# Shift and scale columns of w_ada in two halves, x normed by row before it is transposed, and the scan's state part summed by token

## The chip, the cores and the metric

The program runs on one core of a Trainium2 chip. The metric is the device time of one execution, in microseconds (us); lower is better. The engines are TensorE (PE, with its weight loads as PEld), VectorE (DVE), ScalarE (ACT), GpSimd (POOL) and SyncE (SP, which here issues most transfers).

## The reference, cut to what matters

One layer of a diffusion backbone: 512 latent tokens `x` and 256 context tokens `ctx`, width 1024.

```python
def _rmsnorm(x, g):
    xf = xf * lax.rsqrt(jnp.mean(xf * xf, axis=-1, keepdims=True) + NORM_EPS)
    return xf * g
def _modulate(x, g, shift, scale):
    return _rmsnorm(x, g) * (1 + scale) + shift
...
sh1, sc1, ga1, sh2, sc2, ga2 = split(silu(c) @ w_ada + b_ada, 6)      # and csh1, csc1, ... from c_ctx
p  = _modulate(x,   n_pre_mix, sh1,  sc1)  @ w_in      # q, k, v, z, xbc, dt, gates
pc = _modulate(ctx, n_pre_mix, csh1, csc1) @ w_in
...
# SSD scan, both directions, per group g of 8 heads, chunks c of 128 tokens:
y_diag = einsum('bcgls,bcgrls,bcsgrp->bclgrp', cb, Lm, x)             # inside a chunk
y_off  = einsum('bclgn,bcgrpn,bcgrl->bclgrp', Cc, h_prev, exp(a_cs))  # from the state
y = y_diag + y_off
```

The scan is followed by neighbourhood attention, two branch projections merged by gates, an output projection with a gated residual, and 16 routed SwiGLU experts with a second gated residual. Everything is float32.

## The kernel before, in words

**Tiling.** Products of the projections run as three float32r passes: each operand is cut into a high and a low part (`hh`, `hl` for the latent tokens, `ch`, `cl` for the context, `wh`, `wl` for the weights), and `gemm_k` adds high x high, low x high and high x low over 8 steps k of 128 channels into a PSUM tile of one output tile (128 columns of `w_in` by 512 tokens, or by 256 of the context).

**The opening.** The first lines load x and ctx (`load_xin`, six tiles of 128 tokens), the parts of `w_ada` that hold shift and scale (`load_ada`, 8 tiles q of 128 channels each) and the first columns of `w_in` (`load_first`: dt with 64 columns, B and C with 128). The string START is the order in which SP issues them: x, a and f for the three. NXIN and NWADA are the buffers of the first two. A row of x in SBUF stands in the scan's order of tokens, made by the load (`x_src`). The constants `cn` and the vectors `vec` come over POOL's queue. Each tile of x is squared and summed by row (L305 on DVE for odd tiles, ACT for even), transposed by PE (L310) and copied into `xT`, channels by tokens. `rsq` makes the reciprocal roots `rsv` by ten small DVE instructions (L183 to L188). Since tokens now lie along the free axis, `rsv` is spread over all partitions by matmuls with a diagonal (L318 to L320) into `rsb`, and POOL multiplies `xT` by it, 16 times (L327 to L329).

Then a loop over q = 0 to 7, the k steps of the first three output tiles: eight matmuls of `silu(c)` with the 256 columns of `w_ada` (L336), a copy (L339), two matmuls that select the rows of c and c_ctx and turn them (L342), bias and scale (L345, L347) into `mod`; DVE applies them to `xT` (L351), ACT casts the high part (L352), DVE subtracts for the low part (L353), and `gemm_k` runs for the three tiles (L214 to L222).

**The scan.** Four groups g of heads, two halves hf of 4 heads, four chunks c. `step_states` makes the states `hp` (PE L580, DVE L582 and L584). `step_chunk` makes one chunk of one half: POOL masks the log decays into `dd` (L595), ACT takes exponentials (L599), PE multiplies C with the states (L603), DVE adds the directions (L606), scales the state part of both into `tt` (L608) and weights the inner part by `cbs` (L610). In the tile `py` of PSUM, PE then adds up four matmuls that turn `tt` by the identity, one per direction and pair of heads (L614), and four of the inner part (L618). ACT copies it (`ys`, L622), and SP stores it. The projections and convolutions of group g + 1 (L481, L489) are mixed with this.

**What sets the order.** A scheduler orders each engine's instructions ahead of the run, from the order in which the program is written, from priorities (`high_priority` with the HP_ constants) and from buffer counts. PSUM has pools `pT` (transposes), `pY` (one buffer), `pS` and `mm`. Each engine then runs its list in order and waits where an operand is not there.

## Time and profile before

| | us |
|---|---|
| median of 3 runs (lowest, highest) | 2117.17 (2114.04, 2117.47) |
| profiled execution, own time | 2113.9 |
| its span | 2111.8 |
| PE busy, share of the span | 1950.3, 92% |
| DVE | 899.1, 43% |
| ACT | 636.6, 30% |
| POOL | 293.4, 14% |

The span is from the first to the last recorded event of the profiled execution; its own time is 2.1 us more. Read by stages, with the time that PE was busy in each:

| stage | from, to | PE busy | granted clock |
|---|---|---|---|
| opening | 0, 40 | 18.57 of 40 | 0.95 |
| | 40, 53 | 9.85 of 13 | 0.50 |
| | 53, 80 | 27.00 of 27 | 1.00 |
| first convolutions | 80, 148 | 65.82 of 68 | 0.97 |
| scan, with later projections | 148, 446 | 294.74 of 298 | 1.00 |
| start of the attention | 446, 480 | 29.89 of 34 | 0.90 |
| attention | 480, 780 | 285.16 of 300 | 1.00 |
| gates, branches, merge | 780, 1090 | 302.49 of 310 | 0.98 |
| experts | 1090, 2111.8 | 916.82 of 1021.8 | 0.95 |

"Busy" says that an engine had an instruction under way, not that it could go no faster. The clock is what the throttle granted TensorE: 1.00 is 2.4 GHz, 0.50 is 1.2 GHz. In the rows, a line with x16 is a group of like instructions with its busy time and the mean of one; in a timeline the first number is the start, the second the time that the group was busy, and the bracket the idle time of the engine ahead of it, with what ended it.

### The profile page before, as it was taken

What the parts mean: (1) busy time and instruction counts of PE and PEld (TensorE: products, weight loads), DVE (VectorE), ACT (ScalarE), POOL (GpSimd) and SP (SyncE); (2) the same over time, 40 slices, a digit from 0 to 9 for tenths busy, and PEclk for the clock granted to TensorE, in tenths of its full rate; (3) what the DMA queues carried; (4) which work ended last, traced back from release to release, by engine and by line L of the source; (5) the groups of instructions that cost most, each with busy time, mean ns of one, the idle gap of its engine ahead of it and who ended that gap; (6) DMA issues with size and microseconds to landing.
All of it is one profiled execution on the core that took longest, in us unless ns stands there. A gap on an engine that the chain in (4) does not pass through costs nothing.

```text
span 2111.8 us, 26456 instructions
## 1 busy us (share of the span) xinstructions
PE 1950.3 (92%) x10643; PEld 1268.6 (60%) x10643; DVE 899.1 (43%) x1612; ACT 636.6 (30%) x1263; POOL 293.4 (14%) x386
## 2 busy tenths in 40 slices
PE   5999999999999999999997899999998989899895
PEld 3777787777777777788887434444444334444342
DVE  5787777746666657743336201111111111111113
ACT  2465556435555554542222011100101001010102
POOL 3032213233343323310000000000000000000001
PEclk8999999999999999999998899999999999999998
DMA  9344234342332334454365799999999999999996
GB/s 242 95 133 140 81 119 145 105 142 93 112 117 100 113 106 155 150 175 132 112 249 208 310 393 423 428 428 427 428 427 427 428 428 427 428 426 428 427 428 252
DMA packets 143226, 548.39 MB, mean 260 GB/s; under 512 B 10520, under 2 KB 96584, under 8 KB 116992
## 3 DMA queue, kind: packets, MB, share of 16 engines
q1 hardware_dynamic: 127648, 490.10, 58.6%
q0 software_dynamic: 15024, 55.29, 7.8%
q8 instruction: 84, 1.38, 0.3%
q10 hardware_dynamic: 432, 1.31, 0.2%
q14 instruction: 38, 0.31, 0.0%
HBM read 529.72 MB, written 16.94 MB: 259 GB/s over the span
## 4 chain that ended last, share of the span: by engine, by line
PE 64%; DMA 12%; DVE 8%; issue 4%; ACT 3%; POOL 1%; DVEq 0%; POOLq 0%; ACTq 0%; SPq 0%
PE pu L1229 17%; DMA wb<-in_w_exp_down 7%; PE pd L1272 6%; PE ps_mm L214 4%; PE ps_mm L215 4%; PE ps_mm L220 4%; PE px L1184 3%; PE px L1279 2%; PE ps_mm L935 2%; PE ps_mm L934 2%; PE ps_mm L933 2%; DMA wc<-in_w_exp_up 2%; PE ps_y L614 1%; PE ps_t L798 1%; DMA wc<-in_w_exp_down 1%
## 5 line engine op out<-in xcount | busy, mean ns | idle before, releaser
L214 PE MATMUL ps_mm<-hh,wh 128*128 128x512 f32 (+1 forms) x648 | 265.8, 410 | 10.0 <-DVE sz L920 7.5
L215 PE MATMUL ps_mm<-hl,wh 128*128 128x512 f32 (+1 forms) x648 | 261.6, 404 | 2.6 <-DVE hl L353 2.6
L220 PE MATMUL ps_mm<-hh,wl 128*128 128x512 f32 (+1 forms) x648 | 261.7, 404 | 0.0
L168 DVE TENSOR_TENSOR wl<-raw,wh 128x1024 fp32r<-128x1024 f32 (+2 forms) x109 | 141.7, 1300 | 197.5 <-ACT wh L167 193.2
L167 ACT CAST wh<-raw 128x1024 fp32r<-128x1024 f32 (+2 forms) x109 | 117.1, 1074 | 196.2 <-PE ps_mm L934 84.7
L1229 PE MATMUL pu<-wb,xg 128*64 128x512 f32 x752 | 170.9, 593 | 0.0
L214 PEld LDWEIGHTS ps_mm<-hh,wh 128*128 128x128 f32 (+1 forms) x648 | 123.4, 190 | 44.8 <-issue 17.0
L1171 DVE SCALAR_TENSOR_TENSOR yo<-pd,gs,yo 64x512 fp32r<-64x512 f32 (+1 forms) x34 | 24.4, 718 | 281.2 <-ACT yo L1169 280.6
L215 PEld LDWEIGHTS ps_mm<-hl,wh 128*128 128x128 f32 (+1 forms) x648 | 123.3, 190 | 20.7 <-DVE hl L353 3.1
L220 PEld LDWEIGHTS ps_mm<-hh,wl 128*128 128x128 f32 (+1 forms) x648 | 123.4, 190 | 16.0 <-issue 0.8
L1229 PEld LDWEIGHTS pu<-wb,xg 128*64 128x64 f32 x752 | 75.5, 137 | 81.4 <-issue 54.3
L1211 POOL DMA_DIRECT2D g<-gain_scr x1 | 0.5, 528 | 868.7 <-PE pu L1229 868.7
L1252 DVE SCALAR_TENSOR_TENSOR hid<-hid,pu 128x512 f32<-128x512 f32 x32 | 22.0, 687 | 224.1 <-ACT hid L1251 224.1
L481 DVE SCALAR_TENSOR_TENSOR cacc<-pad,cwh,cacc 128x772 f32<-128x772 f32 (+1 forms) x96 | 100.4, 1050 | 9.6 <-ACT cacc L479 8.6
L1251 ACT ACTIVATE hid<-pu 128x512 f32<-128x512 f32 x32 | 19.0, 597 | 257.8 <-PE pu L1229 257.8
L1169 ACT ACTIVATE yo<-pd,gs 64x512 fp32r<-64x512 f32 (+1 forms) x34 | 22.3, 657 | 232.7 <-PE pd L1272 208.9
L1272 PE MATMUL pd<-wb,hidT 128*64 128x512 f32 x352 | 79.8, 597 | 12.9 <-DMA wb<-in_w_exp_down 12.9
L1279 PE MATMUL px<-yo,ohT 128*128 128x512 f32 x120 | 57.0, 577 | 35.0 <-DVE yo L1171 34.6
L217 PE MATMUL ps_mm<-ch,wh 128*128 128x256 f32 x280 | 82.2, 293 | 4.1 <-ACT rw L684 4.0
L599 ACT ACTIVATE dd<-dd,lnb 128x128 f32<-128x128 f32 x256 | 79.7, 392 | 10.3 <-POOL dd L595 9.9
L222 PE MATMUL ps_mm<-ch,wl 128*128 128x256 f32 x280 | 81.0, 289 | 0.0
L218 PE MATMUL ps_mm<-cl,wh 128*128 128x256 f32 x280 | 80.7, 288 | 0.0
(837 smaller groups left out, 3717.5 us busy)
## 6 DMA issues: line engine op xcount, KB each, us to landing
wb<-in_w_exp_gate SPq DMA_DIRECT2D x31, 2048.0 KB
wb<-in_w_exp_down SPq DMA_DIRECT2D x22, 2048.0 KB
raw<-in_w_in SPq DMA_DIRECT2D x36, 1024.0 KB
wa<-in_w_exp_gate SPq DMA_DIRECT2D x16, 2048.0 KB
wc<-in_w_exp_up SPq DMA_DIRECT2D x16, 2048.0 KB
ws<-in_w_exp_gate SPq DMA_DIRECT2D x16, 2048.0 KB
wr<-in_w_exp_up SPq DMA_DIRECT2D x16, 2048.0 KB
wb<-in_w_exp_up SPq DMA_DIRECT2D x16, 2048.0 KB
```

The lines of the kernel that those rows point to most:

```text
L167: S.copy(wh, v[:, :, c0:c0 + n])
L168: eng.tensor_tensor(wl, v[:, :, c0:c0 + n], wh.bitcast(F32), op=OP.subtract)
L214: PE.matmul(lat, wh[:, k, :m], hh[:, k, :], start=s, stop=False)
L215: PE.matmul(lat, wh[:, k, :m], hl[:, k, :], start=False, stop=False)
L217: PE.matmul(ctxp, wh[:, k, :m], ch[:, k, :], start=s, stop=False)
L218: PE.matmul(ctxp, wh[:, k, :m], cl[:, k, :], start=False, stop=False)
L220: PE.matmul(lat, wl[:, k, :m], hh[:, k, :], start=False, stop=e)
L222: PE.matmul(ctxp, wl[:, k, :m], ch[:, k, :], start=False, stop=e)
L481: E.scalar_tensor_tensor(acc[:, :n], pad[:, j:j + n], w(j), acc[:, :n], op0=OP.mult, op1=OP.add)
L1229: PE.matmul(acc[q * 2 + b][o * 64:(o + 1) * 64, :], xe[:, k, :], w[:, f:f + 512], start=(k == 0), stop=(k == KT - 1))
L1272: PE.matmul(pd[dh * 64:(dh + 1) * 64, :], l, wd[:, q * 1024 + dh * 512:q * 1024 + (dh + 1) * 512], start=(n == 0), stop=(n == 15))
L1279: PE.matmul(p, ohT[:, i * 128:(i + 1) * 128], yo[:, dh], start=True, stop=True)
```

## The change

It has two parts.

**Opening.** x is loaded in token order, one transfer per tile; `vec` and `cn` come over ACT's queue. Of the two halves u of the channels (512 each) `load_ada` fetches 8 tiles, with rows of 512 columns (2 KB) in place of 128 (512 B), each tile two k steps deep. The x tiles are scaled by `rsv` by row, in pairs, before their transposes (DVE even, ACT odd tiles); `rsb`, its diagonals and POOL's multiplies are gone. `columns(u)` makes `mod` for four q at a time, at q = 0 and q = 4: 16 matmuls with 512 columns into one tile of `pY`, one copy, four selecting matmuls, bias and scale. The scan's order of tokens is now made where DVE applies the modulation (a new tile `hq`); ACT applies that of the context.

**Scan.** DVE adds the two directions of `tt`, PE transposes the sum into a tile of its own (`pt`, pool `pT`), `py` holds the inner part alone, ACT copies `pt` into `ys` and DVE adds `py` to it.

```diff
-NXIN = 4
-NWADA = 6
-START = "xxxxafxxafafaaaaa"
+NXIN = 6
+NWADA = 5
+START = "xxxxxxaaaafffaaaa"
...
-    G.dma_start(vec, a["vec"])
-    G.dma_start(cn, a["cn"])
+    S.dma_start(vec, a["vec"])
+    S.dma_start(cn, a["cn"])
...
-        if i < 4:
-            for q in range(2):
-                nc.sync.dma_start(t[q * 64:(q + 1) * 64, :], x_src[2 * i + q])
...
+        nc.sync.dma_start(t, a["x"][i * 128:(i + 1) * 128, :] if i < 4 else a["ctx"][(i - 4) * 128:(i - 3) * 128, :])
...
-    def load_ada(q):
-        r = st.tile([128, KT, 2, 128], F32, name="wada", tag="wada", bufs=NWADA)
+    def load_ada(n):
+        u, k = n // 4, n % 4 * 2
+        r = st.tile([128, 2, 2, 512], F32, name="wada", tag="wada", bufs=NWADA)
         for v in range(2):
-            nc.sync.dma_start(r[:, :, v, :], a["w_ada"][:, v * 1024 + q * 128:v * 1024 + (q + 1) * 128]
+            nc.sync.dma_start(r[:, :, v, :], a["w_ada"][k * 128:(k + 2) * 128, v * 1024 + u * 512:v * 1024 + (u + 1) * 512]
                               .rearrange("(k p) n -> p k n", p=128))
...
-    V.tensor_copy(cb[:, 0:128], ident)
...
-    for i0, n in ((0, 4), (4, 2)):
-        rsq(rsv[:, i0:i0 + n], ssq[:, i0:i0 + n], 1.0 / D, EPS, st)
-        p = pT((128, n * 128))
-        for i in range(n):
-            dg = st.tile([128, 128], F32, name="dg", tag="dg", bufs=2)
-            V.tensor_scalar(dg, ident, rsv[:, i0 + i:i0 + i + 1], None, op0=OP.mult)
-            PE.matmul(p[:, i * 128:(i + 1) * 128], ones, dg, start=True, stop=True)
-        S.copy(rsb[:, i0 * 128:(i0 + n) * 128], p)
+        if i % 2 == 0:
+            continue
+        rsq(rsv[:, i - 1:i + 1], ssq[:, i - 1:i + 1], 1.0 / D, EPS, st)
+        for j in (i - 1, i):
+            if j % 2:
+                S.activation(xin[j], xin[j], AF.Copy, scale=rsv[:, j:j + 1])
+            else:
+                V.tensor_scalar(xin[j], xin[j], rsv[:, j:j + 1], None, op0=OP.mult)
+            for b in range(2):
+                p = pT()
+                for k in range(4):
+                    PE.transpose(p[:, k * 128:(k + 1) * 128], xin[j][:, (b * 4 + k) * 128:(b * 4 + k + 1) * 128], ident)
+                d = xT[:, b * 4:(b + 1) * 4, j * 128:(j + 1) * 128]
+                (S.copy if b else V.tensor_copy)(d, p.rearrange("p (k n) -> p k n", k=4))
...
-    for k in range(KT):
-        for sl in (slice(0, T), slice(T, T + TC)):
-            G.tensor_tensor(xT[:, k, sl], xT[:, k, sl], rsb[:, sl], op=OP.mult)
...
+    def columns(u):
+        with tc.high_priority(offset=HP_ADA):
+            p = pY()
+            for k in range(KT):
+                for v in range(2):
+                    i = k % 2 * 2 + v
+                    PE.matmul(p[i * 32:(i + 1) * 32, :], sil[:, k, :], wada[u * 4 + k // 2][:, k % 2, v],
+                              start=(k < 2), stop=(k >= 6))
+            row = st.tile([128, 512], F32, name="row", tag="row", bufs=1)
+            S.copy(row, p)
+            p = pT((128, 4, 2, 2))
+            for b in range(4):
+                PE.matmul(p[:, b].rearrange("p s v -> p (s v)"), row[:, b * 128:(b + 1) * 128], cn[:, C_SEL:C_SEL + 4],
+                          start=True, stop=True)
...
     for q in range(KT):
...
+        if q % 4 == 0:
+            columns(q // 4)
         for v, sl, hi, lo in ((0, slice(0, T), hh, hl), (1, slice(T, T + TC), ch, cl)):
...
-            V.tensor_scalar(t, t, sc_, sh_, op0=OP.mult, op1=OP.add)
+            if v == 0:
+                t = st.tile([128, T], F32, name="hq", tag="hq", bufs=2)
+                V.tensor_scalar(split_hrc(t), perm_hrc(src), sc_, sh_, op0=OP.mult, op1=OP.add)
+            else:
+                t = src
+                S.activation(t, src, AF.Identity, scale=sc_, bias=sh_)
...
+            V.tensor_tensor(tt[:, 0], tt[:, 0], tt[:, 1], op=OP.add)
+            pt = pT((128, 2, 128))
+            for pr in range(2):
+                PE.transpose(pt[:, pr, :], tt[:, 0, pr * 2:pr * 2 + 2, :].rearrange("p h e -> p (h e)"), ident)
             py = pY((128, 2, 128))
             for pr in range(2):
-                for d in range(2):
-                    PE.matmul(py[:, pr, :], tt[:, d, pr * 2:pr * 2 + 2, :].rearrange("p h e -> p (h e)"), ident,
-                              start=(d == 0), stop=False)
                 for o in range(2):
...
-                              start=False, stop=True)
+                              start=True, stop=True)
             ys = sdl.tile([128, 2, 128], F32, name="ys", tag="ys", bufs=2)
-            S.copy(ys, py)
+            S.copy(ys, pt)
+            V.tensor_tensor(ys, ys, py, op=OP.add)
```

Two places show how the order of the instructions moves. The first is PE's list from its start to the first matmul of the projection (L214). Before, with L310 the transposes, L319 the diagonals, L336 the columns and L342 the selection:

```order
L310 MATMUL ps_t<-cn,xin 128x128 x32
L336 MATMUL ps_y<-wada,sil 32x256 x8
L310 MATMUL ps_t<-cn,xin 128x128 x16
L319 MATMUL ps_t<-dg,cn 128x128 x4
L336 MATMUL ps_y<-wada,sil 32x256 x8
L319 MATMUL ps_t<-dg,cn 128x128
L342 MATMUL ps_t<-cn,row 128x2 x2
```

After, from the last transposes (L311) on, with L330 the columns and L336 the selection:

```order
L311 MATMUL ps_t<-cn,xin 128x128 x8
L330 MATMUL ps_y<-wada,sil 32x512 x4
L336 MATMUL ps_t<-cn,row 128x4 x4
L330 MATMUL ps_y<-wada,sil 32x512
L214 MATMUL ps_mm<-hh,wh 64x512
```

The columns of the first half are finished and selected in one piece, ahead of the projection. Those of the second half are strewn between its first steps; their four selecting matmuls stand once more, ahead of the fifth step.

The second place is PE's list at the first chunks of the scan. Before, L603 is C with the states, L614 and L618 fill `py`:

```order
L603 MATMUL ps_s<-hp,cT 128x256 x3
L222 MATMUL ps_mm<-ch,wl 128x256
L614 MATMUL ps_y<-cn,dd 128x128 x2
L618 MATMUL ps_y<-dd,xs_tok 64x128 x2
L614 MATMUL ps_y<-cn,dd 128x128 x2
L618 MATMUL ps_y<-dd,xs_tok 64x128 x2
L603 MATMUL ps_s<-hp,cT 128x256 x2
```

After, L624 are the two transposes, L629 the inner part, L613 C with the states:

```order
L214 MATMUL ps_mm<-hh,wh 128x512
L624 MATMUL ps_t<-cn,dd 128x128 x2
L215 MATMUL ps_mm<-hl,wh 128x512
L217 MATMUL ps_mm<-ch,wh 128x256
L613 MATMUL ps_s<-hp,cT 128x256 x2
L218 MATMUL ps_mm<-cl,wh 128x256
L220 MATMUL ps_mm<-hh,wl 128x512
L222 MATMUL ps_mm<-ch,wl 128x256
L629 MATMUL ps_y<-dd,xs_tok 64x128
L624 MATMUL ps_t<-cn,dd 128x128 x2
L629 MATMUL ps_y<-dd,xs_tok 64x128 x3
```

Where a chunk's eight matmuls stood in one piece, matmuls of a projection now stand between transposes and inner part. On DVE, at the same place, the new additions are L621 (the directions) and L634 (`ys` and `py`); L168 is the weights' low part, L491 a convolution step, L618 the scaling of the state part:

```order
L491 SCALAR_TENSOR_TENSOR cacc<-pad_621,cwh,cacc 128x772
L618 TENSOR_TENSOR dd<-ps_s,e_tok 128x512
L168 TENSOR_TENSOR wl<-raw,wh 128x1024
L621 TENSOR_TENSOR dd<-dd 128x256
L618 TENSOR_TENSOR dd<-ps_s,e_tok 128x512
L491 SCALAR_TENSOR_TENSOR cacc<-pad_621,cwh,cacc 128x772
L634 TENSOR_TENSOR ys<-ys,ps_y 128x256
L621 TENSOR_TENSOR dd<-dd 128x256
```

The addition that frees `py` (L634) stands behind a convolution step and a weight's low part, one chunk's scaling after the addition of the directions.

## Rows read from the trace of the kernel before

**Rows 1.** Page, part 2: traffic in 40 equal slices of the span.
```profile
GB/s 242 95 133 140 81 119 145 105 142 93 112 117 100 113 106 155 150 175 132 112 249 208 310 393 423 428 428 427 428 427 427 428 428 427 428 426 428 427 428 252
```
**Rows 2.** Windows by stage: from:to, length, then as in the first line.
```profile
core 0: us, PE busy (x) PEld busy (x) DVE busy (x) ACT busy (x) POOL busy (x), PEclk, DMA share, GB/s
40.00:53.00 13.00, 9.85 (x40) 6.23 (x41) 12.82 (x14) 3.82 (x8) 12.87 (x18) 0.50 1.14 290
53.00:80.00 27.00, 27.00 (x201) 18.75 (x199) 14.50 (x36) 9.44 (x21) 0.00 (x0) 1.00 0.43 125
...
148.00:446.00 298.00, 294.74 (x1715) 236.21 (x1714) 219.42 (x299) 165.65 (x409) 79.58 (x108) 1.00 0.34 112
...
2072.00:2084.00 12.00, 10.27 (x83) 5.95 (x78) 1.91 (x4) 3.57 (x6) 0.00 (x0) 1.00 1.04 387
```
**Rows 3.** Timeline of the opening: start, busy us, engine, line [idle before].
```profile
34.37 18.28 POOL L329 TENSOR_TENSOR xT<-xT,rsb 128x512 f32<-128x512 f32 x16 [31.86 <-DVE nw L187]
...
40.32 0.69 PE L214 MATMUL ps_mm<-hh,wh 128*64 128x512 f32 x1 [2.46 <-ACT hh L352]
...
79.84 0.40 PE L220 MATMUL ps_mm<-hh,wl 128*128 128x512 f32 x1
```
**Rows 4.** DVE's groups, 0 to 81 us: count | busy, mean ns | idle before.
```profile
L351 DVE TENSOR_SCALAR xT<-xT,mod 128x512 f32<-128x512 f32 x8 | 6.0, 744 | 1.0 <-DVE mod L345 0.5
...
L312 DVE COPY xT<-ps_t 128x512 f32<-128x512 f32 x6 | 4.1, 688 | 4.2 <-PE ps_t L310 4.2
...
L305 DVE CUSTOM_DVE_ANT_0 scrv<-xin 128x1024 bf16<-128x1024 f32 x3 | 3.7, 1223 | 3.0 <-DMA xin<-in_x 3.0
...
L188 DVE SCALAR_TENSOR_TENSOR rsv<-nw,rsv 128x4 f32<-128x4 f32 x3 | 0.5, 162 | 0.1
...
L305 DVE DVE_READ_ACCUMULATOR2_ANT ssq<- 128x1 f32 x3 | 0.2, 83 | 0.0
```
**Rows 5.** Timeline of DVE and PE between 58 and 76 us.
```profile
58.16 1.07 PE L336 MATMUL ps_y<-wada,sil 128*32 128x256 f32 x16
...
60.97 0.87 DVE L351 TENSOR_SCALAR xT<-xT,mod 128x512 f32<-128x512 f32 x2
...
72.74 0.40 PE L214 MATMUL ps_mm<-hh,wh 128*128 128x512 f32 x1
...
75.53 0.40 PE L214 MATMUL ps_mm<-hh,wh 128*128 128x512 f32 x1
```
**Rows 6.** PE's timeline: one chunk of the scan, and four transposes of the attention.
```profile
174.29 0.71 PE L614 MATMUL ps_y<-cn,dd 128*128 128x128 f32 x4
174.93 0.44 PE L618 MATMUL ps_y<-dd,xs_tok 128*64 128x128 f32 x4
...
494.27 0.60 PE L798 MATMUL ps_t<-cn,s__4326 128*128 128x128 f32 x4
494.62 0.48 PE L220 MATMUL ps_mm<-hh,wl 128*128 128x512 f32 x1
```
**Rows 7.** Groups of the scan, 148 to 446 us.
```profile
L595 POOL TENSOR_SCALAR_AFFINE_SELECT dd<-bc 128x512 f32<-128x512 f32 x60 | 42.6, 729 | 109.5 <-PE ps_y L618 95.9 <-ACT dd L599 4.1 <-DVE dd L608 3.7
...
L168 DVE TENSOR_TENSOR wl<-raw,wh 128x1024 fp32r<-128x1024 f32 x21 | 27.0, 1284 | 14.3 <-ACT wh L167 10.2 <-PE ps_s L603 3.9
...
L582 DVE TENSOR_TENSOR hp<-hp,dec 128x256 f32<-128x256 f32 x42 | 21.1, 508 | 1.8 <-ACT hp L576 1.7
...
L584 DVE TENSOR_TENSOR hp<-hp,ps_s 128x256 f32<-128x256 f32 x42 | 17.0, 411 | 1.1 <-PE ps_s L580 0.7
```
**Rows 8.** Windows in and ahead of the scan, columns as in rows 2.
```profile
130.00:140.00 10.00, 8.18 (x40) 7.17 (x40) 8.89 (x15) 6.48 (x18) 1.26 (x3) 0.83 0.50 158
...
170.00:180.00 10.00, 10.00 (x64) 7.88 (x63) 3.49 (x7) 3.93 (x13) 3.07 (x6) 1.00 0.19 63
...
330.00:340.00 10.00, 9.71 (x48) 7.60 (x47) 10.00 (x18) 5.49 (x14) 2.23 (x3) 1.00 0.40 129
```
**Rows 9.** Timeline at 414 us: POOL's multiply and a DVE multiply beside it.
```profile
414.25 1.47 POOL L564 TENSOR_TENSOR xw<-xs_tok,w_tok 128x512 f32<-128x512 f32 x1
...
414.74 1.26 DVE L582 TENSOR_TENSOR hp<-hp,dec 128x256 f32<-128x256 f32 x1
```
**Rows 10.** PE's timeline at 132 us, ahead of the scan.
```profile
131.82 1.11 PE L489 MATMUL ps_t<-cn,xo 128*128 128x128 f32 x4 [2.07 <-DVE xo L483]
```
**Rows 11.** PE's waits, 148 to 446 us: total, times, longest.
```profile
PE ps_y L614 <- DVE dd L608: 0.7, 1, 0.7
```

More of the change, by code (lines that the diff above doesn't have):

```diff
@@ L74 @@
     0, 16, 32, 40, 160, 184, 200, 216, 280, 344, 472, 480)
[L76 removed]
+C_ID, C_TF, C_TB, C_SF, C_SB, C_ONE, C_IOTA, C_SEL, C_END = 0, 128, 256, 384, 512, 640, 768, 832, 836
 A_COS, A_SIN, A_M, A_END = 0, 512, 1024, 1024 + 3 * 256
@@ L297, in emit @@
     xT = st.tile([128, KT, T + TC], F32, name="xT")
-    rsb = st.tile([128, T + TC], F32, name="rsb")
     for i in range(6):
@@ L326, in emit @@
         tiles0.append((wh, wl, mm((w, T)), pS((w, TC)) if n < 2 else None, w))
-    for k in range(KT):
-        for sl in (slice(0, T), slice(T, T + TC)):
-            G.tensor_tensor(xT[:, k, sl], xT[:, k, sl], rsb[:, sl], op=OP.mult)
     mod = st.tile([128, KT, 2, 2], F32, name="mod")
-    for q in range(KT):
-        with tc.high_priority(offset=HP_ADA):
-            p = pY((128, 256))
-            for k in range(KT):
-                i = k % 4
-                PE.matmul(p[i * 32:(i + 1) * 32, :], sil[:, k, :], wada[q][:, k].rearrange("p v n -> p (v n)"),
-                          start=(k < 4), stop=(k >= 4))
-            row = st.tile([128, 256], F32, name="row", tag="row", bufs=2)
-            S.copy(row, p)
-            p = pT((128, 2, 2))
-            for i in range(2):
-                PE.matmul(p[:, i, :], row[:, i * 128:(i + 1) * 128], cn[:, C_SEL:C_SEL + 2], start=True, stop=True)
-            m = mod[:, q]
-            b2 = vec[:, V_BADA + q:V_BADA + q + 1]
-            V.tensor_tensor(m, p, bass.AP(tensor=b2.tensor, offset=b2.offset, ap=[list(b2.ap[0]), [8, 2], [0, 2]]), op=OP.add)
-            g = vec[:, V_GPRE + q:V_GPRE + q + 1]
-            V.tensor_scalar(m[:, 1], m[:, 1], 1.0, g, op0=OP.add, op1=OP.mult)
-        for v, sl, hi, lo in ((0, slice(0, T), hh, hl), (1, slice(T, T + TC), ch, cl)):
-            t, hi, lo = xT[:, q, sl], hi[:, q, :], lo[:, q, :]
-            sh_, sc_ = m[:, 0, v:v + 1], m[:, 1, v:v + 1]
-            V.tensor_scalar(t, t, sc_, sh_, op0=OP.mult, op1=OP.add)
@@ new lines, in columns @@
+    def columns(u):
[12 more added lines that the diff above has]
+                          start=True, stop=True)
+            m = mod[:, u * 4:(u + 1) * 4]
+            b2 = vec[:, V_BADA + u * 4:V_BADA + u * 4 + 1]
+            V.tensor_tensor(m, p, bass.AP(tensor=b2.tensor, offset=b2.offset, ap=[list(b2.ap[0]), [1, 4], [8, 2], [0, 2]]),
+                            op=OP.add)
+            V.scalar_tensor_tensor(m[:, :, 1], m[:, :, 1], 1.0, vec[:, V_GPRE + u * 4:V_GPRE + u * 4 + 4]
+                                   .rearrange("p (k o) -> p k o", o=1).to_broadcast([128, 4, 2]), op0=OP.add, op1=OP.mult)
@@ new lines, in emit @@
+    for q in range(KT):
+        if q % 4 == 0:
+            columns(q // 4)
+        for v, sl, hi, lo in ((0, slice(0, T), hh, hl), (1, slice(T, T + TC), ch, cl)):
+            src, hi, lo = xT[:, q, sl], hi[:, q, :], lo[:, q, :]
+            sh_, sc_ = mod[:, q, 0, v:v + 1], mod[:, q, 1, v:v + 1]
+            if v == 0:
[4 more added lines that the diff above has]
+                S.activation(t, src, AF.Identity, scale=sc_, bias=sh_)
@@ L370, in emit @@
     sk, es_sk = pool("sk", side="right")
+    V.tensor_copy(cb[:, 0:128], ident)
+    V.tensor_copy(cb[:, 128:256], ones)
+    V.tensor_copy(cb[:, 256:384], cn[:, C_SB:C_SB + 128])
     dts, es_dts = pool("dts", side="right")
@@ L1337, in constants @@
     cn[:, C_IOTA:C_IOTA + 64] = np.arange(1, 65)[None, :]
-    cn[:, C_SEL:C_SEL + 2] = i[:, None] % 32 == np.arange(2)[None, :]
+    cn[:, C_SEL:C_SEL + 4] = i[:, None] % 64 == np.array([0, 1, 32, 33])[None, :]
     ac = np.zeros((128, A_END), np.float32)
```

11 lines of the change are left out of this document (removed).

## The prediction

> **What bounds the kernel now.** I read the profile from coarse to fine. The line of the 40 slices that tells the traffic comes first [rows 1]: from slice 24 on it stands at 423 to 428 GB/s, so the second half (the experts) moves weights at one steady rate, and nothing in this change touches it. An earlier end of the first half moves it earlier as a whole, since its loads wait for tiles that the first half holds. The change touches two stages, which the windows show [rows 2]. In the **opening**, up to 80 us, the reader is to see that PE works at a granted clock of 0.50 (1.2 GHz) from 40 to 53, with VectorE (DVE) and GpSimd (POOL) both full, and at 1.00 (2.4 GHz) from 53 to 80 without a gap. In the **scan**, 148 to 446, PE is busy 294.7 of 298 us and DVE 219.4: PE sets the pace there, and DVE has a quarter in hand. The timeline of the opening [rows 3] tells what set its start: POOL's 16 multiplies by the row norm run from 34.37 for 18.28 us, the first matmul of the projection stands at 40.32, the last starts at 79.84 and ends at 80.2.
>
> **The change, the opening.** It removes POOL's 18.28 us and the diagonal matmuls (L318 to L320). x is scaled by row instead, ahead of its transposes, so the norm is done before anything waits for it. The path is then x landed, DVE's chain, the columns of w_ada, the first matmul.
> Landing: x, ctx, cn and vec are 3.7 MB, the first half of w_ada 4 MB. Its rows of 512 B came at 290 GB/s between 40 and 53; late in the program, where rows of 2 KB are loaded, 387 stand [rows 2]. 7.7 MB take 20 to 26.5 us, and from a start at 2 us the first half is there at 22 to 28.5.
> DVE's chain, from the second tile of x (some 6 us): three squares of 1.30 with their read, six copies of 0.69, three chains of ten small instructions of 0.16 that I space by 0.2 (6.0 us), and three scalings of 128x1024. Beside a busy POOL 128x512 took 0.74 [rows 4]; with POOL idle, 512 and 256 columns together took 0.87, so 1024 take some 1.2 [rows 5]. 3.9 + 4.1 + 6.0 + 3.6 = 17.6, so 24 us [rows 4]. Both ends meet. The last four column matmuls (about 1.0 at full clock, as 16 pieces of half the width have now [rows 5]; 2 at half), copy, four selecting matmuls, two small DVE steps, the first scaling and cast: some 6 us, so the first matmul stands at 30 (27 to 34) in place of 40.3. Waits on ScalarE (ACT) for its casts are counted in.
> From there PE does eight k steps of 2.79 us each at full clock (72.74 to 75.53 [rows 5]), 22.3 in all, and the second half of the columns, four groups of 1.0 (8 groups of 1.07 before, the same work). Before, PE stayed at 0.50 for some 12 us after its first matmul [rows 2]; I take 11 here, which do 2 steps in place of 4. So 30 + 11 + 2 x 2.79 + 4 x 1.0 = 50.6. Here the change adds a wait: all four later k steps need mod of the second half, which is made in one lump, and in PE's order the selecting matmuls come right behind the first four steps. Copy, select, add, scale and cast take some 3 us with PE idle, then 4 x 2.79 = 11.2: the last matmul ends at about 65 against 80.2. The bounds are 60 (no stretch at half clock) and 72 (all four first steps at half clock, columns at 290 GB/s). Of the 15 I leave one for casts that PE may wait for between the first steps, and take a gain of **14**, bounds 8 to 20.
> At nothing I cost: vec and cn issued by ACT in place of POOL (both stand ahead of ACT's first work on x), the cb casts (still at the head of DVE's order), the ctx half scaled by ACT (ACT is busy 9.4 of 27 us in that stretch [rows 2]), and SP's queue, whose 16 w_ada transfers have a quarter of the rows.
>
> **The change, the scan.** Each of 32 chunks loses four 128x128 matmuls by the identity: on PE two of them, in four pieces, hold it from 174.29 to 174.93, 0.64 us, so 1.28 per chunk [rows 6]. It gains two transposes: four took from 494.27 to 494.62, so 0.18 for two [rows 6]. 32 x 1.10 = 35 us at these rows; where other work stands between the pieces they weigh less on PE, so I take 31. ACT copies as before, from another tile. DVE gains two instructions per chunk: an addition of two SBUF tiles (128x256) and one with PSUM. The nearest rows are 508 and 411 ns [rows 7]: 32 x 0.92 = 29 us more on DVE.
> So within 298 us PE's work goes from 295 to 264, and DVE's from 219 to 249. If PE stays the bound, the scan gains 31; if DVE and PE share it without slack between them, nothing like that. Two things speak for a good part: the new additions fall in the stretches where chunks are worked off, and there DVE is free (3.49 of 10 us at 170 to 180 [rows 8]); and PE has matmuls of the next projection between the steps. Against: in its order DVE has long steps between the two halves of a chunk (a weight split of 1.28 [rows 7], conv steps), and ps_y has one buffer, which now is given back by DVE's addition, behind them, not by ACT's copy. Split and the two additions alone are 1.28 + 0.51 + 0.41 = 2.2 us, and the products of the chunk, PE's transposes and ACT's copy stand between them: some 4 us. PE has about 3 us of other matmuls there by its order (its list after the change, at the first chunks). I charge half of the 1 us that is left over, 0.5 per chunk: 16 of the 31. A gain of **15 to 16**, bounds 0 and 31.
> On the first of these additions the trace shows a second price: a 128x256 step of the same form took 1.26 us where POOL's multiply ran beside it, against a mean of 0.508 over 42 of them [rows 7, 9]. The Trainium skill's page SBUF — State Buffer, section Who interferes with whom, has the rule for it: a VectorE instruction with two SBUF inputs contends with a GpSimd one that reads SBUF, and the loser waits for the whole instruction. The rows agree. By that rule, at its worst, each of the 32 additions would wait for one of POOL's selections (0.73 us [rows 7]), 23 us more on DVE, and the scan would gain next to nothing, which is the first rival below. I don't take it: a selection writes the tile that the chunk before last has left, so by the program it runs mostly behind these additions, not beside them.
>
> **Sum.** 14 + 16 = 30 us. The profiled execution took 2113.9 (span 2111.8 and 2.1 around it); 30 less is 2084. The median of the runs is 3.3 above it, 2117.2, so I give **2087**.
>
> **The rivals.**
> (1) *DVE takes PE's place in the scan.* Its 249 us and most of its idle time (298 - 219 = 79 before, waits for exponentials and for PE) fill the old 298. For it: stretches with DVE at 10 of 10, as 330 to 340 [rows 8]. Against: most chunks lie in others. The opening's 14 remain: 2103.
> (2) *The opening gains nothing.* The lump of columns comes late, or PE starts earlier only to be held at half clock longer; what then stands at 80 stands there again. For it: 12 us at 0.50 before. Against: POOL's 18 us are gone whatever the clock does. The scan's 16 remain: 2101.
> (3) *Slower: PE waits for DVE's release of ps_y in every chunk.* Where no other work stands before the waiting matmul, PE loses the DVE steps ahead of the addition, up to some 4 us as above, and a gap of 2.07 us before L489 stands in ten us in which the mean clock is 0.83 [rows 8, 10]. It decides against the change from (31 + 14) / 32 = 1.4 us per chunk; at 2 us it is 2117 - 14 - 31 + 64 = 2136. Against it: the one wait of this kind in the trace of before, PE on DVE's product, is 0.7 us in all [rows 11].
>
> **How the numbers follow.** The forecast has 0.62, with a spread of its own from 2069 (20 and 28 gained) to 2101 (8 and 8). Rival 1 has 0.17, rival 2 0.08, rival 3 0.06; 0.07 is for both stages giving nothing, 2113 to 2120. The range 2069 to 2108 holds the forecast and rivals 1 and 2 with their middles and leaves out rival 3, the nothing, and some of each edge. Within 0.2% is 4.2 us about 2117, which is about what a measurement of this kernel can tell from no change. Faster by more: nearly all of the first three, 0.86; within: 0.07; slower, rival 3 and a little of the nothing: 0.07.
>
> **What would show it.** In the profile after: no POOL row before the pads; first L214 near 30, last of the projection near 65, PEclk 0.50 for about ten us from the first one. A first matmul behind 36 makes the opening's step wrong; a clock that stays at 0.50 until the second half, the clock term. In the scan PE's busy share falls from 99% to some 94%, DVE's rises to 88%; its length is 280 or so. PE rows at the chunk's matmuls with idle time put down to DVE's addition size the 0.5 us per chunk: more than 1.4 us is rival 3, and none with the length unchanged is rival 1. Should the stages behind the scan change their lengths, the sum is wrong in its ground.

## The result, and the profile after

The changed kernel takes **2077.06 us** (median of 4 runs, 2074.90 to 2080.12) against 2117.32 (4 runs, 2114.04 to 2118.97): 40 us less. The ratio is 0.981 by these medians; its estimate is 0.982, with a 95% interval of 0.9803 to 0.9836. The forecast was 2087, range 2069 to 2108: direction and range held, and the gain was 40 in place of 30. The stages show that the two terms of the sum were both wrong, in opposite directions.

Start times of the same instructions in four traces, two of each kernel (the second pair was made later, on another occasion):

| start, us | before | after | before, again | after, again |
|---|---|---|---|---|
| first matmul of the projection | 40.3 | 34.8 | 43.8 | 34.8 |
| first transpose behind the opening's projection | 80.2 | 72.6 | 82.0 | 72.7 |
| last matmul of the last chunk | 445.1 | 414.4 | 445.3 | 413.5 |
| first scores of the attention | 487.2 | 452.5 | 486.4 | 450.2 |
| last norm of the gates | 890.8 | 853.9 | 891.5 | 848.2 |
| transposes of the router | 1151.3 | 1113.0 | 1153.8 | 1107.9 |
| last output matmul | 2096.9 | 2061.6 | 2102.6 | 2053.1 |

In the first pair the opening is 7.6 us ahead at its end, the scan adds 23.1, the passage to the attention 4.0. Behind that come 2.2 up to the gates and 1.4 up to the router; the experts give 3.0 back at the very end. In the second pair the opening is 9.3 ahead, since the kernel before ended its opening at 80.2 in one trace and at 82.0 in the other; the scan adds 22.5 there, and the passage 4.4.

The opening after, timeline of PE (start, busy us; L330 columns, L336 selection, L214 first pass of the projection):

```profile
21.11 1.05 PE L330 MATMUL ps_y<-wada,sil 128*32 128x512 f32 x2
...
22.89 1.06 PE L330 MATMUL ps_y<-wada,sil 128*32 128x512 f32 x6
...
28.48 1.06 PE L330 MATMUL ps_y<-wada,sil 128*32 128x512 f32 x8
30.25 1.05 PE L336 MATMUL ps_t<-cn,row 128*128 128x4 f32 x8 [0.71 <-ACT row L333]
...
34.76 0.69 PE L214 MATMUL ps_mm<-hh,wh 128*64 128x512 f32 x1 [2.47 <-ACT wh L167]
...
43.67 1.04 PE L330 MATMUL ps_y<-wada,sil 128*32 128x512 f32 x2
...
45.66 1.06 PE L330 MATMUL ps_y<-wada,sil 128*32 128x512 f32 x6
...
56.75 0.95 PE L336 MATMUL ps_t<-cn,row 128*128 128x4 f32 x8
59.80 0.68 PE L214 MATMUL ps_mm<-hh,wh 128*64 128x512 f32 x2 [2.10 <-ACT hh L358]
...
72.32 0.40 PE L220 MATMUL ps_mm<-hh,wl 128*128 128x512 f32 x1
```

The reader is to see four things beside [rows 3, 5]. A matmul stands here in two pieces, so x2 is one matmul, x6 are three, and x8 is a whole group of four. The first matmul of the projection waits for ACT's cast of the *weights* (L167), not of x. The second half's columns come as x2 and x6, and both take the time of x8. The selection stands behind the fourth step, with 2.10 us of idle time behind it. And two groups of the first half are split in the same way (at 21.11 and 22.89, and once more at 24.69 and 26.47), between the last transposes. PE is busy there for 9.31 of 10 us, and DVE's last copies of the transposed x wait for it:

```profile
20.00:30.00 10.00, 9.31 (x57) 3.98 (x55) 4.07 (x9) 4.35 (x7) 0.17 (x3) 1.00 1.11 328
```
```profile
26.14 0.69 DVE L313 COPY xT<-ps_t 128x512 f32<-128x512 f32 x1 [2.45 <-PE ps_t L311]
28.15 0.69 DVE L313 COPY xT<-ps_t 128x512 f32<-128x512 f32 x1 [1.32 <-PE ps_t L311]
```

The clock in the same stretch, windows (columns as in rows 2):

```profile
35.00:40.00 5.00, 5.00 (x17) 3.59 (x17) 5.00 (x10) 4.75 (x9) 0.00 (x0) 0.50 1.05 375
40.00:45.00 5.00, 5.00 (x22) 2.42 (x21) 1.01 (x3) 0.00 (x0) 0.00 (x0) 0.96 1.10 344
...
60.00:65.30 5.30, 5.30 (x22) 3.89 (x22) 4.67 (x11) 3.77 (x10) 0.00 (x0) 0.68 0.02 5
```

PE works at 0.50 for five to six us after its first matmul, where [rows 2] had 13, and a second time for a few us behind the idle time of the lump. The stretch from the end of the opening to the last chunk, before and after:

```profile
80.20:445.10 364.90, 359.46 (x2086) 290.98 (x2085) 280.41 (x376) 204.95 (x481) 95.92 (x127) 1.00 0.35 112
```
```profile
72.60:414.40 341.80, 335.28 (x1902) 268.04 (x1902) 302.60 (x439) 202.83 (x482) 101.00 (x125) 1.00 0.38 119
```

PE is as full as ever (98%), in 23 us less; DVE has 22 us more. Of PE's work, the matmuls by the identity alone (L614, before) and the two transposes that replace them (L624, after), from the windows of these lines:

```profile
80.20:487.20 407.00, 43.39 (x256) 34.33 (x256) 0.99 0.37 119
```
```profile
72.60:452.50 379.90, 13.04 (x64) 6.87 (x64) 0.99 0.40 127
```

43.4 - 13.0 = 30.4 us less of PE's time; 27.1 of it is seen in the length up to the first scores (407.0 to 379.9). PE's busy time in all fell by 26.9 over that stretch (397.45 to 370.57, sums of its two windows): the rows of one line count ends that overlap other matmuls. PE's waits in the scan after (total, times, longest), to be read against [rows 11]:

```profile
PE ps_t L499 <- DVE xo L493: 3.0, 4, 2.1
PE ps_t L624 <- DVE dd L621: 1.1, 3, 0.5
PE ps_y L629 <- DVE dd L620: 1.0, 2, 0.8
PE ps_s L584 <- DVE dd L618: 0.4, 2, 0.2
PE ps_s L613 <- DVE hp L594: 0.4, 1, 0.4
```

None of the 32 releases of `ps_y` by DVE's addition (L634) stands there. The rows of DVE's two additions (window from 140 to 415) show who waits instead: DVE, 9.6 us in all, for ACT's copies.

```profile
L621 DVE TENSOR_TENSOR dd<-dd 128x256 f32<-128x256 f32 x32 | 15.3, 481 | 0.3
L634 DVE TENSOR_TENSOR ys<-ys,ps_y 128x256 f32<-128x256 f32 x32 | 13.4, 419 | 10.0 <-ACT ys L633 9.6
```

### The profile page after: what moved, and what is told of

It is laid out like the page before. It is cut to its first block, busy times and chain, and to the rows that moved or that the text cites. A ratio compares the mean times of both kernels' runs of the same rounds, so it can differ in the third digit from the quotient of the medians.

```text
span 2077.1 us, 25937 instructions
## 1 busy us (share of the span) xinstructions
PE 1925.2 (93%) x10359; PEld 1237.4 (60%) x10359; DVE 906.8 (44%) x1665; ACT 638.6 (31%) x1266; POOL 281.3 (14%) x368
## 4 chain that ended last, share of the span: by engine, by line
PE 58%; DMA 10%; DVE 8%; issue 5%; ACT 2%; POOL 2%; DVEq 0%; ACTq 0%; POOLq 0%
PE pu L1241 18%; DMA wb<-in_w_exp_down 7%; PE pd L1284 7%; PE px L1196 3%; PE ps_mm L214 3%; PE ps_mm L220 3%; PE ps_mm L215 3%; PE px L1291 2%; PE ps_mm L946 2%; PE ps_mm L945 2%; PE ps_mm L947 2%; DMA wc<-in_w_exp_up 2%; PE ps_t L810 1%; PE ps_y L820 1%; PE ps_s L796 1%
## 5 line engine op out<-in xcount | busy, mean ns | idle before, releaser
L214 PE MATMUL ps_mm<-hh,wh 128*128 128x512 f32 (+1 forms) x648 | 265.6, 410 | 10.9 <-DVE sz L932 6.4
L168 DVE TENSOR_TENSOR wl<-raw,wh 128x1024 fp32r<-128x1024 f32 (+2 forms) x109 | 139.6, 1280 | 188.1 <-ACT wh L167 187.9
L167 ACT CAST wh<-raw 128x1024 fp32r<-128x1024 f32 (+2 forms) x109 | 117.1, 1075 | 191.0 <-PE ps_mm L946 84.4
L214 PEld LDWEIGHTS ps_mm<-hh,wh 128*128 128x128 f32 (+1 forms) x648 | 123.0, 190 | 47.1 <-issue 16.6
L491 DVE SCALAR_TENSOR_TENSOR cacc<-pad,cwh,cacc 128x772 f32<-128x772 f32 (+1 forms) x96 | 97.3, 1018 | 1.0 <-ACT cacc L489 0.5
L1291 PE MATMUL px<-yo,ohT 128*128 128x512 f32 x120 | 59.2, 594 | 34.8 <-DVE yo L1183 34.3
## 6 DMA issues: line engine op xcount, KB each, us to landing
wb<-in_w_exp_gate SPq DMA_DIRECT2D x31, 2048.0 KB, 29.3
ws<-in_w_exp_gate SPq DMA_DIRECT2D x16, 2048.0 KB, 27.1
```

The lines of the kernel that those rows point to most:

```text
L167: S.copy(wh, v[:, :, c0:c0 + n])
L168: eng.tensor_tensor(wl, v[:, :, c0:c0 + n], wh.bitcast(F32), op=OP.subtract)
L214: PE.matmul(lat, wh[:, k, :m], hh[:, k, :], start=s, stop=False)
L491: E.scalar_tensor_tensor(acc[:, :n], pad[:, j:j + n], w(j), acc[:, :n], op0=OP.mult, op1=OP.add)
L1291: PE.matmul(p, ohT[:, i * 128:(i + 1) * 128], yo[:, dh], start=True, stop=True)
```

## The experiments

All times are medians of 4 to 6 runs beside runs of the kernel before on the same chip; the ratio is to these. Their medians lie between 2114.2 and 2115.7 (2117.3 beside the changed kernel), so between two rows of this table 2 or 3 us say nothing, and the starts of the stages say more.

| run | what | us | ratio, 95% | opening's end | last chunk |
|---|---|---|---|---|---|
| after | | 2077.06 | 0.982 (0.9803, 0.9836) | 72.6 | 414.4 |
| e1_opening | opening alone | 2103.1 | 0.9935 (0.9922, 0.9947) | 71.9 | 436.8 |
| e2_scan | scan alone | 2087.52 | 0.9872 (0.9855, 0.989) | 80.9 | 421.0 |
| e3_together | after, columns in fours | 2067.85 | 0.9774 (0.9759, 0.9789) | 65.3 | 407.5 |
| e4_sum_only | after, sum by DVE, turned by identity | 2092.3 | 0.9885 (0.9868, 0.9902) | 72.4 | 426.4 |
| e5_dve_more | after, one more DVE step a chunk | 2083.88 | 0.9846 (0.9832, 0.9859) | 71.0 | 415.8 |
| e5c_dve_more3 | after, three more | 2081.39 | 0.9841 (0.9827, 0.9854) | 71.2 | 417.1 |
| e6_by_row_only | after, columns by q as before | 2066.06 | 0.9768 (0.9755, 0.9781) | 65.7 | 407.4 |
| e7_weights_early | e6, first weights loaded earlier | 2065.05 | 0.9767 (0.975, 0.9785) | 65.6 | 406.1 |
| e8_split4 | e3, first weights loaded earlier | 2068.46 | 0.978 (0.9761, 0.9799) | 62.9 | 403.6 |

### Each part alone

The opening alone: the changed kernel with the chunk as it was.

```diff
-            V.tensor_tensor(tt[:, 0], tt[:, 0], tt[:, 1], op=OP.add)
-            pt = pT((128, 2, 128))
...
+                for d in range(2):
+                    PE.matmul(py[:, pr, :], tt[:, d, pr * 2:pr * 2 + 2, :].rearrange("p h e -> p (h e)"), ident,
+                              start=(d == 0), stop=False)
...
-            V.tensor_tensor(ys, ys, py, op=OP.add)
```

> The changed kernel with the scan's state part as it was before (four matmuls by the identity per chunk, ACT copies py): the opening's part of the change alone. Theory, from the two traces: the opening moved the first transposes of the first convolution (L489 before, L499 after) from 114.0 to 106.5 us, and nothing behind it gives that back, so about 7.5 us are gained: 2109 to 2111. Rival, the forecast's term of 14: 2103. The scan's length should be that of before, 298 us from 148 on.

The scan alone is the kernel before with the opposite edit.

> The kernel before with only the scan's state part changed (sum by token, two transposes, DVE adds py). Theory, from the two traces: the last chunk moved by 30.7 us, 7.5 of them from the opening, so 23 in the scan, and 4 more up to the first scores of the attention, because some matmuls of the projection now run inside the scan's stretch: 27 us, 2088 to 2092. Rival, the forecast's term of 16: 2101. Together with the run of the opening alone the gains should add up to 35 to 40; more or less would show that the two parts depend on each other.

The scan alone came out as expected, 2087.5 (28 us less than the 2115.7 beside it). From the opening's end to the last chunk it takes 340.1 us, the changed kernel 341.8, before 364.9. The opening alone took 2103.1, 12.6 less than the 2115.7, where I had expected 2109 to 2111: its opening did give only 8.3 (80.2 to 71.9), the scan was 364.9 as before, but 6.3 more appeared between the attention and the gates, a stage that no edit touches. The two gains add up to 41, against 40 for both together, though half of the first came from that untouched stage. By the stages it is 8.3 in the opening and 24.8 in the scan, against 7.6 to 9.3 and 22.5 to 23.1 together: no dependence of the parts on each other is to be seen.

### The columns of the opening

Only the inner loop's order is changed, so that the four matmuls on the four 32-column groups of PE (i = 0 to 3) wait for the same transfer:

```diff
-                for v in range(2):
+                for v in (1, 0):
                     i = k % 2 * 2 + v
```

> The changed kernel with the inner loop of the column matmuls in the order v = 1, 0, so that the first of each group of four waits for the transfer that lands last and the four stand together in PE's list (x4 in place of 1 and 3). Theory: four matmuls on the four quarters of PE run side by side (one group 1.06 us), a lone one takes as long as three (1.04 and 1.06), so the second half of the columns costs 4 x 2.1 us when it is split in 1 and 3, and 4 x 1.06 together: the end of the opening's projection moves from 72.7 to about 68.5, 4 us earlier, 2073. Rival: the second half is held by its transfers, the last columns stay near 55 and the end near 72.7: no change, 2077.

2067.85, with the opening's end at 65.3 in place of 72.6: more than expected. PE's timeline:

```profile
26.12 1.92 PE L330 MATMUL ps_y<-wada,sil 128*32 128x512 f32 x16
...
32.43 0.69 PE L214 MATMUL ps_mm<-hh,wh 128*64 128x512 f32 x1 [2.62 <-ACT hh L358]
...
40.59 1.06 PE L330 MATMUL ps_y<-wada,sil 128*32 128x512 f32 x8
...
47.52 1.07 PE L330 MATMUL ps_y<-wada,sil 128*32 128x512 f32 x8
...
49.44 0.95 PE L336 MATMUL ps_t<-cn,row 128*128 128x4 f32 x8
...
52.49 1.11 PE L214 MATMUL ps_mm<-hh,wh 128*64 128x512 f32 x2 [1.53 <-ACT hh L358]
```

A whole group of four takes 1.06 to 1.07, as long as one of the four alone in the changed kernel (1.04): the first matmul comes 2.3 us earlier, and the second selection 7.3. On what lies behind this the Trainium skill's page TensorE: Matmul & The Clock Gate, in its Part 3 on packing small matmuls, says that small matmuls whose outputs start at different 32-partition strips run side by side in the array. The rows agree, and add that side by side in the code is not enough: the scheduler had put another matmul between them, since the first needed one transfer and the other three a second one.

Then the columns as before the change, made by q from rows of 512 B, with all the rest as changed:

```diff
-    def load_ada(n):
-        u, k = n // 4, n % 4 * 2
-        r = st.tile([128, 2, 2, 512], F32, name="wada", tag="wada", bufs=NWADA)
+    def load_ada(q):
+        r = st.tile([128, KT, 2, 128], F32, name="wada", tag="wada", bufs=NWADA)
...
-        if q % 4 == 0:
-            columns(q // 4)
...
+            p = pY((128, 256))
...
+                PE.matmul(p[i * 32:(i + 1) * 32, :], sil[:, k, :], wada[q][:, k].rearrange("p v n -> p (v n)"),
+                          start=(k < 4), stop=(k >= 4))
```

> The changed kernel with the columns of w_ada as before: eight tiles in rows of 512 B, columns, selection and mod made for one q at a time (all else as changed: x normed by row, token order, the scan). Theory, what cost the opening its gain is the lump and the split groups of the columns, not the rows: with a first matmul at 32 to 34, eight steps of 2.79 (22.3), four groups of columns (1.07 and a selection each, 5) and 3 to 5 us lost at half clock, the projection ends at 62 to 66, in place of 72.6: 2067 to 2071. Rival, the rows of 512 B at 290 GB/s set the time: the tiles of q 4 to 7 land at 41 and behind, each step waits, the end is at 72 or later: 2077 or more.

2066.06, end of the opening at 65.7. The slow rows are there; windows of that run:

```profile
30.00:35.00 5.00, 2.02 (x21) 1.28 (x18) 4.58 (x13) 4.90 (x12) 0.00 (x0) 0.71 1.03 273
35.00:40.00 5.00, 5.00 (x18) 3.71 (x19) 4.06 (x6) 2.60 (x4) 0.00 (x0) 0.61 1.15 292
```

273 to 292 GB/s, against 375 in the changed kernel. The Trainium skill's page Perfetto Trace Analysis, section DMA Optimizations, says that transfers in small pieces (under 2 KB) carry a large overhead and should be made larger. The rate agrees. The time does not follow it: behind its first matmul PE has no idle time in that run (10.00 of 10 us busy from 40 to 50 and again from 50 to 60).

The run undoes two things at once, though. It has no lump, and by q its groups of four stand together (x16 pieces of half the width in 1.07 us; one of the eight is split), as they do in e3_together. That run keeps the lump and the rows of 2 KB, and ends its opening at 65.3, this one at 65.7. So the 6.9 us by which this run is ahead of the changed kernel there (72.6 to 65.7) are the price of the split groups, and not of the halves: with whole groups, lump and larger rows come out even with columns by q.

That run's first matmul waited for weights, so their loads were moved up:

```diff
-START = "xxxxxxaaaafffaaaa"
+START = "xxxxxxafafafaaaaa"
```

> The kernel with x normed by row, columns by q in rows of 512 B and the changed scan (the run of the row norm alone), with the first weights of the projection loaded between the first tiles of w_ada (start order x6, then a f a f a f a a a a a). In that run the first matmul, at 34.9 us, waited for ACT's cast of the first weights at 34.3, while the first high part of x was ready at 30.3. Theory: the first matmul moves to 31 to 32, the end of the projection from 65.7 to 62 to 63, 2062 to 2064. Rival: the 1.3 MB of weights push the columns back by as much, and the end stays at 65 to 67: 2065 to 2068.

The first matmul came 5.6 us earlier, and the end did not move at all (65.7 to 65.6). Timeline and windows of that run:

```profile
29.30 0.69 PE L214 MATMUL ps_mm<-hh,wh 128*64 128x512 f32 x1 [1.36 <-ACT hh L348]
```
```profile
30.00:35.00 5.00, 5.00 (x28) 3.23 (x29) 2.23 (x6) 1.75 (x5) 0.00 (x0) 0.50 1.17 294
35.00:40.00 5.00, 5.00 (x31) 3.36 (x29) 3.10 (x6) 2.36 (x4) 0.00 (x0) 0.66 1.12 285
```

PE is busy without a gap from 30 to 40 and works at 0.50 for most of it, up to 38.4, which is 9.1 us; in the run without the earlier weights it idled up to 35 and came back to full clock at 38.6, after 3.7 us at 0.50. What PE does in 5.4 us more at half clock would take 2.7 at full clock, so the clock took back about half of the gain. The other half is order: that run had four of its eight groups of columns done before its first matmul, this one two, and the other two, with their selections, take some 2.7 us behind it. So the weights' position was right as a cause, and the end came where the rival had put it.

> The changed kernel with the columns' groups of four together and the first weights loaded between the tiles of w_ada (start order x6, a a f a a f f a a a a). In the run with the groups together the first matmul, at 32.4 us, waited for the first high part of x, not for weights. Theory: with the weights ahead of it nothing is gained at the start, and the columns of the first half come up to 2 us later: end of the projection 65 to 68, 2067 to 2070. Rival: ACT, relieved of the weights' casts at 33 to 36, lets the second to fourth step come earlier: end at 63 to 65, 2064 to 2067.

This is e3_together (columns in two halves, whole groups) with the first weights loaded between the tiles of w_ada. Its opening ends at 62.9, 2.4 before that of e3_together, with the first matmul at 32.4 in both. That is the end that the rival had forecast; that ACT's relief is its cause was not taken apart. It is also 2.7 before the end of e7_weights_early, which has columns by q, but the weights stand elsewhere in its start order. In the time (2068.46 against 2067.85 and 2065.05) this is not to be seen.

### What sets the pace of the scan

The state part summed by DVE, but turned as before, by matmuls with the identity into `py`; ACT copies `py`:

```diff
-            pt = pT((128, 2, 128))
-            for pr in range(2):
-                PE.transpose(pt[:, pr, :], tt[:, 0, pr * 2:pr * 2 + 2, :].rearrange("p h e -> p (h e)"), ident)
...
+                PE.matmul(py[:, pr, :], tt[:, 0, pr * 2:pr * 2 + 2, :].rearrange("p h e -> p (h e)"), ident,
+                          start=True, stop=False)
...
-            S.copy(ys, pt)
-            V.tensor_tensor(ys, ys, py, op=OP.add)
+            S.copy(ys, py)
```

> The changed kernel, but the state part, summed by token, is turned by two matmuls by the identity that accumulate in py with the inner part, and ACT copies py: DVE's second addition and the transposes are left out. Theory, PE sets the pace of the scan: two such matmuls cost 4 pieces of 0.147 us, 18.9 us over 32 chunks, the two transposes 9.2 (both from issue to issue in the traces), so this is 10 us slower than the changed kernel: 2087. Rival, DVE sets the pace, as the forecast's charge of 0.5 us a chunk has it: DVE is spared 13.4 us and its wait for ACT's copy, 9.6, so it is as fast or faster: 2065 to 2077.

2092.3, 15 us slower than the changed kernel, though DVE has 13.4 us less to do and never waits for that copy. PE's time in these 64 matmuls (128 pieces), window of the line:

```profile
72.40:469.40 397.00, 28.35 (x128) 20.55 (x128) 0.99 0.39 122
```

28.35 against 13.04 for the transposes: 15.3 us, where the stretch up to the first scores grew by 17.1 (379.9 to 397.0). PE's busy time in all grew by 12.9 over it (370.57 to 383.45); the rest are waits, most of them for ACT behind the last chunk. PE sets the pace of the scan. The size was off because I had taken half of the old 37.7 us from issue to issue; in these rows a matmul costs more with half as many of them (0.44 us against 0.34), and why was not looked into.

Then DVE was loaded further, with one and with three multiplications by 1 ahead of the addition that gives `ps_y` back:

```diff
+            V.tensor_scalar(ys, ys, 1.0, None, op0=OP.mult)
             V.tensor_tensor(ys, ys, py, op=OP.add)
```

> The changed kernel with one more DVE step per chunk, a multiplication of ys by 1 ahead of the addition that gives ps_y back (128x256, some 0.35 us, 11 us over 32 chunks). DVE was busy 241.7 of 274.8 us of the scan in the changed kernel. Theory, PE sets the pace and DVE's idle time takes it up: within 4 us of the changed kernel, 2077 to 2081, the scan's end by at most 4 us later. Rival, each delay of the release of ps_y or of DVE is passed on to PE (the forecast's 0.5 us a chunk): 11 us or more, 2088 and up.

> The same with three such steps per chunk, some 34 us more on DVE: 276 us of work where the scan takes 275. Theory: DVE becomes the bound, and what exceeds its idle time lengthens the scan, 10 to 34 us: 2087 to 2111. Should it stay within 5 us of the changed kernel, DVE's steps overlap more than the busy time tells.

With three (group and window of that run, from the opening's end to the last chunk):

```profile
L635 DVE TENSOR_SCALAR ys<-ys 128x256 f32<-128x256 f32 x93 | 36.5, 404 | 2.0 <-ACT ys L633 1.5
```
```profile
71.20:417.10 345.90, 335.39 (x1911) 270.26 (x1912) 327.51 (x533) 205.65 (x484) 106.00 (x125) 1.00 0.37 118
```

The new rows sum to 36.5 us, and as steps overlap at their ends DVE's busy time rose by 24.9 (302.60 to 327.51), to 95% of this stretch. The stretch became 4.1 us longer (341.8 to 345.9; 344.8 with one step). Both runs are 4 to 7 us slower as a whole, and three steps are no slower than one: behind the scan the one with a single step lost 6 us between the last chunk and the first scores (44.1 against 38.1), where PE waited 3.8 and 2.5 us for ACT. So the first expectation missed in the total, the second missed too (DVE did not become the bound), and what both were to tell apart is told: DVE's slack takes up most of what is put on it.

### Scatter, and two stages that were not touched

> The kernel before, unchanged, profiled a second time. Question: two stages behind the scan differ between the traces though no line of theirs was changed. From the end of the attention to the last norm of the gates before took 109.3 us, the changed kernel 106.9, the opening's part alone 103.1; and the last matmuls of the experts (9.8 us at granted clock 1.00 before) took 12.9 in the changed kernel at 0.74. If these belong to the change, the second trace of before repeats 109 and 9.8; if they are scatter between executions, it gives other values, between 103 and 109 and up to 14.

> The changed kernel, unchanged, profiled a second time. If the two stages belong to the change, 106.9 and 12.9 us again; if they are scatter, other values. The opening and the scan should repeat: end of the projection at 72.6, last chunk at 414.4, first scores at 452.5, each within 1 us or so.

The last matmuls, from the first to the last output, in before, before again, after, after again:

```profile
2075.20:2096.90 21.70, 18.30 (x145) 11.29 (x144) 5.62 (x14) 6.74 (x15) 4.99 (x4) 1.00 0.60 222
```
```profile
2077.80:2102.60 24.80, 21.39 (x145) 12.46 (x144) 5.62 (x14) 6.71 (x15) 5.04 (x4) 0.86 0.54 202
```
```profile
2036.90:2061.60 24.70, 21.29 (x144) 12.41 (x144) 5.58 (x14) 6.70 (x15) 5.04 (x4) 0.86 0.54 198
```
```profile
2031.50:2053.10 21.60, 18.19 (x144) 11.22 (x144) 5.56 (x14) 6.71 (x15) 4.99 (x4) 1.00 0.61 227
```

Both kernels have both values, some 21.7 at clock 1.00 and some 24.8 at 0.86: scatter between executions, worth 3 us. It is part of why the spans of the first pair of traces differ by 34.7 us, those of the second by 48.9, and the medians by 40. The gates are another matter. From the end of the attention to their last norm before took 109.3 and 109.6, the changed kernel 106.9 and 103.5, and the nine other variants 103.0 to 107.0. PE's wait there, in the same order:

```profile
PE ps_mm L214 <- DVE sz L920: 7.5, 2, 4.8
```
```profile
PE ps_mm L214 <- DVE sz L920: 7.3, 2, 4.7
```
```profile
PE ps_mm L214 <- DVE sz L932: 6.4, 2, 4.3
```
```profile
PE ps_mm L214 <- DVE sz L932: 4.0, 2, 2.2
```

Both traces of the changed kernel wait less for `sz`, by 1.1 and 3.3 us, and the stage is shorter by 2.4 and 6.1. Why is not settled: the code of the stage is the same, and no run here takes it apart.

## Why the prediction was right, and where it was wrong

**The ground held, but for one stage.** The attention and the experts moved as a whole; PE sets the pace of the scan; the experts' 427 GB/s took over earlier. The gates became shorter, which by the prediction's own sign is a fault in its ground. The sum was 30 us and 40 came: in the first pair of traces the opening gave 6 less than its term, the scan 11 more, and some 4 more came from the gates.

**The opening: 14 forecast, 7.6 measured at its end in the first pair of traces and 9.3 in the second, about its lower bound of 8.** By its steps, in the first trace of the changed kernel:
- *Landing* was right. From 0 to 20 us 7.0 MB came in (314 and 389 GB/s in the two halves), so the 7.7 MB were there near 22.
- *DVE's chain*, forecast to end at 24, is the step that failed, and with it the first matmul: 30 (27 to 34) forecast, 34.8 measured. The chain added up DVE's own work, as if PE's part in it took no time. The scalings by row were early (the last at 21.7; 0.75 each in place of 1.2), but the chain's last copy ended at 28.8. DVE's copies waited 4.6 us for PE's transposes, and PE was full with these and with the first half's columns, two groups of which were split and cost 2.1 us more for it.
- *From the last columns to the first matmul*: "some 6 us" forecast, 6.3 measured (28.48 to 34.76), although the weights' cast came 1.3 us behind that of x. e3_together takes 2.3 us of the 4.8 back: its last transposes end near 26 in place of 28.5, and the weights' cast no longer comes last. There too the last copy ends at 26.5 and not at 24.
- *Clock*: 11 us at half clock were charged and 5 to 6 came, a gain of some 2.5; but a second stretch, behind the lump, was not in the sum (60 to 65.3 at 0.68, some 1.7 us lost).
- *Second half of the columns*: 4 x 1.0 forecast, 4 x (1.04 + 1.06) = 8.4 measured; one of the pieces of 1.04 fell in PE's wait ahead of the first matmul, the other 7.4 us stand behind it. Beside DVE's chain this is the term that was most wrong. I had read "the same work" from [rows 5], where 16 pieces stand together, and had before me the order in which the groups were strewn, without giving it a price.
- *Lump*: 3 us of idle time forecast; 0.95 of selection and 2.10 of waiting, right. What the lump costs against columns made q by q was a question that the prediction did not ask. With whole groups it costs nothing: 65.3 in e3_together, 65.7 in e6_by_row_only.

**The scan: 16 forecast, 27 measured, inside its bounds of 0 and 31.** PE's saving of 31 was close (30.4 by the rows of the two lines, 26.9 in PE's busy time in all). The step that failed is the charge of 0.5 us per chunk for DVE's late release of `ps_y`: PE's waits in that stretch grew from 4.9 to 5.9 us in all, 1 us in place of 16. Of the signs that the prediction named, DVE's 88% came (241.73 of 274.80 us, from 140.5 to 415.3), and PE's 94% did not (98%). The estimate of 4 us for the way from the sum to the release was set against 3 us of other matmuls, chunk by chunk; but PE's list goes on with the projection and the next group's states, and DVE had a quarter of the stage in hand. Even three more steps a chunk on that very path, 24.9 us of DVE's busy time, cost 4.1.

**The rivals.** (1), DVE takes PE's place, did not happen: e5c_dve_more3 puts 24.9 us on top, e4_sum_only takes 13.4 away, and neither moves the scan as DVE's time would. The second price that the prediction tied to it did come, but seldom: L621 takes 0.418 as a rule, and 6 of its 32 instances, each beside an instruction of POOL, took 0.53 to 1.27 us. That is 2 us in all, in place of 23 at worst. The longest, with POOL's multiply beside it:

```profile
384.60 1.29 POOL L574 TENSOR_TENSOR xw<-xs_tok,w_tok 128x512 f32<-128x512 f32 x1 [2.05 <-PE ps_s L584]
```
```profile
384.91 1.27 DVE L621 TENSOR_TENSOR dd<-dd 128x256 f32<-128x256 f32 x1
```

So the rule of the Trainium skill's page SBUF — State Buffer, section Who interferes with whom, on two SBUF inputs beside GpSimd agrees with this trace too.

(2), PE starts earlier and is held at half clock longer, is not what the change did (5 to 6 us at 0.50 in place of 13). e7_weights_early shows the mechanism: of a start 5.6 us earlier nothing was left at the end, and half of it went to the clock. (3), PE waits for `ps_y`, has no row at all.

**The rest.** 3.6 us between the first scores and the router in the first pair of traces, 9.7 in the second, were forecast as none. They lie mostly in the gates (2.4 and 6.1), and their cause stays open.

**Two errors and one range.** The total was right to 10 us because -6 in the opening met +11 in the scan. The range of 2069 to 2108 held it for that reason too.

## What to carry to other kernels

Where small matmuls share PE by column groups, look in the order whether the groups stand together: a group that waits for two transfers is split by the scheduler, and each piece then costs what the whole would; let the first one issued wait for the last transfer. Larger pieces for a transfer were not worth much here, where nobody waited for it: columns in two lumps from rows of 2 KB and columns made one k step at a time from rows of 512 B, at 290 GB/s, ended the opening within 0.4 us of each other. To tell the two apart took a run in which nothing else differed; beside the split groups the halves had looked 7 us too dear. A chain that passes through two engines is to be added up on both. And an engine with a quarter of a stage in hand takes up new steps on a release path nearly free of charge (4 us for 25 here), as long as the waiting engine has other work in its list.
